# Three unused matmuls in the RWKV recurrence, fp32 low-rank weights kept in SBUF, and the low parts' stores moved to another queue

## The chip, the cores and the metric

The kernel runs on one core of one Trainium2 chip. The metric is device time in microseconds (us) of one execution; less is better. The core's engines are named as the profile names them: PE (TensorE; PEld is its weight load), DVE (VectorE), ACT (ScalarE), POOL (GpSimd) and SP (SyncE). ACTq and SPq are the DMA issues of ACT and SP. PEclk is the granted TensorE clock, 1.00 for 2.4 GHz and 0.50 for 1.2 GHz.

## The reference, cut to what matters

The whole is a two-layer decoder: RWKV-7 time mixing, a feed-forward block, sparse attention, another feed-forward block, over 1024 tokens of width 1024, in float32. Only the time mixing is touched:

```python
xm = x[None] + xx[None] * mix[:, None, None, :]
r, k, v = jnp.einsum('nbsd,nde->nbse', xm[:3], w_rkv)
xv, xw, xa, xg = xm[2], xm[3], xm[4], xm[5]
w_log = -jax.nn.softplus(-(w0 + jnp.tanh(xw @ w1) @ w2)) - 0.5
decay = jnp.exp(-jnp.exp(w_log.astype(f32)))
...
a = jax.nn.sigmoid(a0 + (xa @ a1) @ a2)
g = jax.nn.sigmoid(xg @ g1) @ g2
...
def _wkv7_step(state, inp):
    r_t, w_t, k_t, v_t, a_t, b_t = inp
    sa = jnp.einsum('bhvk,bhk->bhv', state, a_t)
    state = (state * w_t[:, :, None, :] + sa[..., None] * b_t[:, :, None, :]
             + v_t[..., None] * k_t[:, :, None, :])
    y = jnp.einsum('bhvk,bhk->bhv', state, r_t)
    return state, y
```

The kernel does the scan in chunks of 64 tokens: inside a chunk the steps become a triangular system, whose 64x64 matrices (one for each head and chunk) are inverted first.

## The kernel before, in words

**Units.** The time mixing (`rwkv`, about the first 1060 us of the execution) works in four units: two halves of the tokens (hf 0 and 1, 512 tokens each) by two halves of the width (g 0 and 1, 512 columns, 8 heads). In this text a unit is written (hf, g), and they run in the order (0,0), (0,1), (1,0), (1,1). A half begins with `load_x` (tokens loaded and transposed) and `lora1` (the first, narrow factors of the low-rank products, fp32 matmuls, L415). A unit then has `lora2` (the second factors, L517 and L518, a sigmoid on each result by ACT, L519), the projections r, k and v (`proj`), the decays, `prep` (chunk matrices), `invert`, and `wkv` (eight chunks of the recurrence). The generator of each stage is interleaved with others, so that a projection of the next unit runs under the inversion and the recurrence of the one before. The framework's scheduler sets the order on each engine from the order in which the code issues and from its own estimate of times; each engine then works through its list strictly in that order.

**Split precision.** A projection multiplies fp32 data as a high and a low part, each fp32r: ACT casts the raw tile to `hi`, and DVE or POOL computes `lo = raw - hi` (`split`, L54 and L60). Three matmuls (L65, L66, L67) of 128x512 make one product, 12 for each of the 8 contraction steps (kt) of a projection. The weights' tiles are called wr (raw), wh and wl, those of the mixed tokens xm, xmh and xml.

**Kept operands.** `pair` (L436 to L452) makes the two parts the first time and stores them to DRAM if they are needed again: the weights' parts when hf = 0 (for half 1), the tokens' parts when g = 0 (for g = 1). Both stores are issued from ACT's queue (L451), the low part's behind the high part's. When they are needed again, two loads from SP's queue (L445) take the place of load, cast and subtraction. wh, wl, xmh, xml and some tiles of `load_x` and `lora1` share one pool of 14 slots of 128x512 (`u`, with `k.NU` as its size); raw weights have 3 slots (`raw`).

**lora2.** In each unit the columns of w2 and a2 that it needs (128x512 each, 256 KB) are loaded through SP and split like any weight, and the small activations were stacked before by `lora1` as high and low parts over 128 partitions (hw and ha, L419 to L426). Sixteen fp32r matmuls follow, 128x512 each.

**invert.** On DVE, `Lt` (128 partitions by 32x32) is eliminated row by row (L655 and L661), 32 steps of two operations between which DVE takes other work. A MEMSET (L662) writes its diagonal. Then, for each of two halves (sub), DVE transposes the blocks (TX, L666 and the next statement), PE multiplies them in 32 small 32x32 matmuls (xps, L678), ACT copies the result, PE does another 32 (tps, L683), and ACT copies that. `wkv` of the unit follows (its matmuls L717 to L744).

The lines which the prediction's steps touch: the store in `pair` (L451), its reload (L445), the raw weights' load (L124), `lora1` from L418 on, `lora2`, the end of `invert` (L662 to L683), and `k.NU` (14).

Of the kernel before, what the change touches and what calls it, by code (L numbers as in the profile page):

```python
# [7 lines left out]
F32 = mybir.dt.float32  # L8
# [37 lines left out]
def f32(ap):  # L46
    return ap.bitcast(F32)
# [259 lines left out]
def rwkv(k, src, dst):  # L307
# [12 lines left out]
    def t(name, dt=F32):  # L320
        return M_.tile([128, 512], dt, name=name, tag="t", bufs=5)
# [31 lines left out]
    SB = [M_.tile([128, 4, 2, 64], F32, name=f"S{g}") for g in range(2)]  # L353
    for z in SB:
        nc.gpsimd.memset(z, 0.0)
    halo = M_.tile([128, 8], F32, name="halo")
    nc.gpsimd.memset(halo, 0.0)
    st = {}
# [39 lines left out]
    def lora1(hf):  # L398
        xT = st[hf]["xT"]
        a = [acc("la") for _ in range(4)]  # L400
        for kt in range(KT):
            xx = t("xx")
            nc.vector.tensor_tensor(xx, xT[:, kt, 0:512], xT[:, kt, 1:513], ALU.subtract)
            w = raw("wl1")[:, :288]
            nc.sync.dma_start(w, k.w_l1[kt * 128 : (kt + 1) * 128, :])
            xm = {}
            for n in (3, 4, 5):
                xm[n] = u("xm")
                c = V_MIX + 8 * n + kt
                nc.vector.scalar_tensor_tensor(  # L410
                    xm[n], xx, k.vec[:, c : c + 1], xT[:, kt, 1:513], ALU.mult, ALU.add
                )

            for b, n, c0, c1, p0 in ((0, 3, 0, 64, 0), (1, 4, 64, 128, 64), (2, 5, 128, 256, 0), (3, 5, 256, 288, 96)):
                nc.tensor.matmul(  # L415
                    a[b][p0 : p0 + c1 - c0], w[:, c0:c1], xm[n], start=kt == 0, stop=kt == KT - 1
                )
        hw = M_.tile([128, 512], F32R, name="hw", tag="hw", bufs=1)  # L418
        tw = t("tw")  # L419
        nc.scalar.activation(tw[:64], a[0][:64], AF.Tanh)  # L420
        nc.scalar.copy(hw[:64], tw[:64])
        nc.vector.tensor_tensor(hw[64:], tw[:64], f32(hw[:64]), ALU.subtract)
        ha = M_.tile([128, 512], F32R, name="ha", tag="ha", bufs=1)
        nc.scalar.copy(ha[64:], a[1][64:])
        nc.vector.tensor_copy(ha[:64], a[1][64:])
        nc.vector.tensor_tensor(ha[64:], a[1][64:], f32(ha[64:]), ALU.subtract)  # L426
        tg = t("tg")
        nc.scalar.activation(tg, a[2], AF.Sigmoid)
        nc.sync.dma_start(gsc[hf, 0:128], tg)
        tg2 = t("tg2")  # L430
        nc.scalar.activation(tg2[96:], a[3][96:], AF.Sigmoid)
        nc.sync.dma_start(gsc[hf, 128:160], tg2[96:])
        st[hf].update(hw=hw, ha=ha)

    ahead = {}
    PF = [CFG['pf0'], CFG['pf1'], CFG['pf2']]  # L436
# [3 lines left out]
    def pair(key, make, again):  # L440

        if key in kept:
            hi, lo = u(key[0] + "h", F32R), u(key[0] + "l", F32R)
            for i, x in enumerate((hi, lo)):
                nc.sync.dma_start(f32(x), kept[key][i])  # L445
            return hi, lo
        hi, lo = make()
        if again:
            kept[key] = DR.tile([2, 128, 512], F32, name="kept_" + "_".join(map(str, key)))
            for i, x in enumerate((hi, lo)):  # L450
                nc.scalar.dma_start(kept[key][i], f32(x))  # L451
        return hi, lo  # L452

    def operands(hf, n, g, kt):
# [45 lines left out]
    def lora2(hf, g):  # L500

        h_ = st[hf]
        AR = P_.tile([128, 4, 1024], F32, name="AR", tag="AR", bufs=2)
        BK = P_.tile([128, 4, 1024], F32, name="BK", tag="BK", bufs=1)
        s = un[hf, g] = dict(AR=AR, BK=BK)
        if CFG["pfl"] == "b":
            prefetch(hf, 0, g, 1)
        w2 = wtile(k.w_w2[:, g * 512 : (g + 1) * 512], lo_eng=CFG["l2"])
        a2 = wtile(k.w_a2[:, g * 512 : (g + 1) * 512], lo_eng=CFG["l2"])
        if CFG["pfl"] == "a":  # L510
            prefetch(hf, 0, g, 1)
        for i in range(4):
            p = 4 * g + i
            sl = slice(i * 128, (i + 1) * 128)
            for o, w, h, v0 in ((v2(BK[:, i, :512]), w2, h_["hw"], V_W0), (slot(AR[:, i], 0), a2, h_["ha"], V_A0)):
                ps = acc("l2")
                nc.tensor.matmul(ps, w[0][:, sl], h, start=True, stop=False)  # L517
                nc.tensor.matmul(ps, w[1][:, sl], h, start=False, stop=True)  # L518
                s["last"] = nc.scalar.activation(o, v2(ps), AF.Sigmoid, bias=k.vec[:, v0 + p : v0 + p + 1])  # L519

    def decays(hf, g):
# [119 lines left out]
    def invert(hf, g):  # L641
# [10 lines left out]
        for j in range(1, 31):  # L652
# [7 lines left out]
            )  # L660
            nc.vector.tensor_tensor(Lt[:, j + 1 :, :j], Lt[:, j + 1 :, :j], tv, ALU.add)  # L661
        nc.vector.memset(Lt.rearrange("p a b -> p (a b)")[:, 0:1024:33], 1.0)  # L662
        for sub in range(2):
            L = Ln[sub]
            TX = w4("TX", [128, 32, 32])
            nc.vector.transpose(  # L666
                TX[64:96].rearrange("p n j -> p j n"), Lt[64 * sub : 64 * sub + 32].rearrange("p i j -> p j i")
            )
            for b in range(2):
                q = slice(64 + 32 * b, 96 + 32 * b)  # L670
                nc.vector.transpose(
                    L[q, :, 32 * b : 32 * b + 32].rearrange("p n i -> p i n"),
                    Lt[64 * sub + 32 * b : 64 * sub + 32 * b + 32],
                )
            for o in (0, 16):
                ps = (mi if o else ud)("xps").rearrange("p (n i) -> p n i", i=32)
                for n in range(16):
                    nc.tensor.matmul(ps[96:, n], L[64:96, o + n, 32:64], TX[64:96, o + n], start=True, stop=True)  # L678
                CP(k, CFG["cT"])(TX[96:, o : o + 16], ps[96:])
            for o in (0, 16):  # L680
                ps = (mi if o else ud)("tps").rearrange("p (n i) -> p n i", i=32)
                for n in range(16):
                    nc.tensor.matmul(ps[64:96, n], TX[96:, o + n], L[96:, o + n, 32:64], start=True, stop=True)  # L683
                CP(k, CFG["cM"])(L[64:96, o : o + 16, 32:64], ps[64:96])
# [1245 lines left out]
def setup(tc, args, es):  # L1930
    k = Ctx()
    k.tc, k.nc = tc, tc.nc
    for n, a in zip(_INS, args):
        setattr(k, n, a)
    k.NU = 14
    k.psum = k.rows = None
    k.dram = es.enter_context(tc.tile_pool(name="scratch", bufs=1, space=bass.MemoryType.DRAM))
    C = es.enter_context(tc.tile_pool(name="consts", bufs=1, reuse_waits="tile"))
    k.ident = C.tile([128, 128], F32, name="ident")
    k.nc.sync.dma_start(k.ident, k.c_ident)  # L1940
    k.vec = C.tile([128, V_END], F32, name="vec")
    k.nc.sync.dma_start(k.vec, k.vecs)
    k.mhalf = C.tile([128, 16], F32, name="mhalf")
    k.nc.gpsimd.memset(k.mhalf, -0.5)
    return k
# [41 lines left out]
```

## Time and profile before

| | us |
|---|---|
| median of three runs | 3228.42 |
| lowest and highest | 3226.88 and 3240.63 |
| the profiled execution, its own time | 3233.26 |
| its span in the trace | 3231.4 |
| PE busy in the span | 2864.5 (89%) |
| DVE, POOL, ACT busy | 2455.2, 1518.1, 1377.4 |

The profiled execution is one run among others; its time is 4.84 us above the median of the three. The granted clock is 0.924 of full speed in the mean. A row of the timeline reads: start, duration (both us), engine, line, operation, output and inputs, shape, count, and in brackets the idle time of the engine before it with what ended that idle time. A busy PE can still be slow, since a stretch at the granted clock 0.50 counts as busy too; so the clock of a stretch is read beside its busy time.

### The profile page before, as it was taken

What the parts mean: (1) busy time and instruction counts of PE and PEld (TensorE: products, weight loads), DVE (VectorE), ACT (ScalarE), POOL (GpSimd) and SP (SyncE); (2) the same over time, 40 slices, a digit from 0 to 9 for tenths busy, and PEclk for the clock granted to TensorE, in tenths of its full rate; (3) what the DMA queues carried; (4) which work ended last, traced back from release to release, by engine and by line L of the source; (5) the groups of instructions that cost most, each with busy time, mean ns of one, the idle gap of its engine ahead of it and who ended that gap; (6) DMA issues with size and microseconds to landing.
All of it is one profiled execution on the core that took longest, in us unless ns stands there. A gap on an engine that the chain in (4) does not pass through costs nothing. (4 is left out here: it accounts for less than half of the span.)

```text
span 3231.4 us, 41664 instructions
## 1 busy us (share of the span) xinstructions
PE 2864.5 (89%) x15032; PEld 2246.0 (70%) x15032; DVE 2455.2 (76%) x3925; ACT 1377.4 (43%) x2363; POOL 1518.1 (47%) x987
## 2 busy tenths in 40 slices
PE   7689889989897899999698888888998899999788
PEld 3468657777675677777576766566787677777577
DVE  5486767766756788888976689997475888888975
ACT  3433234322322544444223577775363544444331
POOL 2433215222144667766767522212313677766766
PEclk9788978879898999999889889999999999999899
DMA  5554533534325222235212521112214222235212
GB/s 178 198 199 141 189 108 113 181 135 161 121 86 179 82 79 79 78 92 207 78 66 73 182 69 54 45 33 101 80 43 163 61 78 79 79 98 202 78 52 91
DMA packets 236224, 356.44 MB, mean 110 GB/s; under 512 B 17290, under 2 KB 110858, under 8 KB 235634
## 3 DMA queue, kind: packets, MB, share of 16 engines
q1 hardware_dynamic: 208370, 303.44, 29.3%
q10 hardware_dynamic: 27648, 50.34, 4.1%
q8 instruction: 118, 1.93, 0.3%
q14 instruction: 88, 0.72, 0.1%
HBM read 250.57 MB, written 103.15 MB: 109 GB/s over the span
## 5 line engine op out<-in xcount | busy, mean ns | idle before, releaser
L60 POOL TENSOR_TENSOR wo<-wr,wo 128x512 fp32r<-128x512 f32 x220 | 410.8, 1891 | 288.8 <-ACT wo L54 288.8
L1050 DVE SCALAR_TENSOR_TENSOR cv<-u,vec,cv 128x1023 f32<-128x1023 f32 (+1 forms) x176 | 348.2, 1996 | 52.9 <-ACT cv L1045 51.1
L65 PE MATMUL dn<-dh 128*128 128x512 f32 x532 | 219.4, 412 | 68.5 <-DVE acc L1177 68.4
L60 POOL TENSOR_TENSOR dl<-raw,dh 128x1024 fp32r<-128x1024 f32 x82 | 221.1, 2719 | 101.4 <-ACT dh L54 101.1
L65 PE MATMUL p<-xT,wo 128*128 128x512 f32 x528 | 213.4, 404 | 25.3 <-ACT u L1034 19.0
L66 PE MATMUL dn<-dl,dh 128*128 128x512 f32 x532 | 218.1, 410 | 15.2 <-POOL dl L60 7.7
L67 PE MATMUL dn<-dh,dl 128*128 128x512 f32 x532 | 215.9, 406 | 0.0
L1045 ACT ACTIVATE cv<-u,vec 128x1024 f32<-128x1024 f32 x88 | 109.5, 1244 | 248.8 <-DVE u L1039 248.2
L1682 POOL TENSOR_TENSOR cm<-sc,toep 128x256 f32<-128x256 f32 x96 | 75.7, 794 | 297.1 <-DVE mn L1698 228.5
L67 PE MATMUL p<-xT,wo 128*128 128x512 f32 x528 | 208.7, 395 | 5.1 <-POOL wo L60 5.1
L66 PE MATMUL p<-xT,wo 128*128 128x512 f32 x528 | 208.6, 395 | 3.0 <-DVE xT L60 3.0
L1177 DVE SCALAR_TENSOR_TENSOR acc<-acc,dn 128x512 f32<-128x512 f32 x196 | 130.8, 679 | 86.7 <-PE dn L67 86.7
L60 POOL TENSOR_TENSOR wo<-S,wo 128x512 fp32r<-128x512 f32 x88 | 175.6, 2014 | 30.3 <-ACT wo L54 30.3
L54 ACT CAST dh<-raw 128x1024 fp32r<-128x1024 f32 x95 | 94.8, 1047 | 198.0 <-PE dn L67 80.7
L65 PEld LDWEIGHTS dn<-dh 128*128 128x128 f32 x532 | 105.7, 199 | 98.0 <-DVE acc L1177 42.5
L60 POOL TENSOR_TENSOR wl<-wr,wh 128x512 fp32r<-128x512 f32 x56 | 76.6, 1367 | 199.2 <-ACT wh L54 118.5
L65 PEld LDWEIGHTS p<-xT,wo 128*128 128x128 f32 x528 | 100.6, 190 | 63.6 <-ACT u L1034 34.2
L65 PE MATMUL p<-x,wo 128*128 128x512 f32 x352 | 138.8, 394 | 2.8 <-DVE x L60 2.3
L54 ACT CAST wo<-wr 128x512 fp32r<-128x512 f32 x220 | 127.0, 618 | 29.1 <-POOL wo L60 18.7
L54 ACT CAST wh<-wr 128x512 fp32r<-128x512 f32 x108 | 66.6, 621 | 169.8 <-DMA wr<-in_w_w_dram 51.6
L66 PE MATMUL p<-x,wo 128*128 128x512 f32 x352 | 138.4, 393 | 0.0
L65 PE MATMUL pa<-xmh,wh 128*128 128x512 f32 x256 | 106.1, 439 | 36.3 <-ACT xmh L54 32.2
(422 smaller groups left out, 8685.9 us busy)
## 6 DMA issues: line engine op xcount, KB each, us to landing
wr<-in_w_up_dram SPq DMA_DIRECT2D x88, 512.0 KB, 5.9
hd<-cv SPq DMA_DIRECT2D x44, 512.0 KB, 3.4
raw<-hd SPq DMA_DIRECT2D x19, 1024.0 KB, 5.0
raw<-in_w_down_dram SPq DMA_DIRECT2D x19, 1024.0 KB, 7.7
wr<-in_w_wo_dram SPq DMA_DIRECT2D x68, 256.0 KB, 2.9
wr<-in_w_rkv_dram SPq DMA_DIRECT2D x48, 256.0 KB, 3.4
kept_w<-wh ACTq DMA_DIRECT2D x48, 256.0 KB, 2.2
kept_w<-wl ACTq DMA_DIRECT2D x48, 256.0 KB, 3.7
```

What stands on the lines that cost most here:

```text
L54: nc.scalar.copy(hi, raw)
L60: eng.tensor_tensor(lo, raw, f32(hi), ALU.subtract)
L65: mm(ps, lhs[0], rhs[0], start=start, stop=False, **kw)
L66: mm(ps, lhs[0], rhs[1], start=False, stop=False, **kw)
L67: mm(ps, lhs[1], rhs[0], start=False, stop=stop, **kw)
L1045: nc.scalar.activation(o, u, AF.Identity, bias=k.vec[:, cb : cb + 1], scale=k.vec[:, cw[2] : cw[2] + 1])
L1050: nc.vector.scalar_tensor_tensor(o[:, d:], u[:, : 1024 - d], k.vec[:, cw[j] : cw[j] + 1], o[:, d:], ALU.mult, ALU.add)
L1177: nc.vector.scalar_tensor_tensor(o, o, ALPHA if first else 1.0, ps, ALU.mult, ALU.add)
L1682: (nc.vector if CFG["cm"][h4] == "v" else nc.gpsimd).tensor_tensor(cm[:, :near], mk, toep[g][:, h % 8, 256 - near :], ALU.add)
```

## The change

It has three parts, all in `rwkv`.

In `invert`, after the MEMSET of the diagonal, three fp32 matmuls of 128x512 multiply a piece of `Lt` with another piece of it, into the PSUM bank that xps takes next. Nothing reads their result. They need only the MEMSET, and xps needs the transposes and the bank.

In `lora1` and `lora2`, w2 and a2 are loaded once, at the start, 64 partitions each, into one fp32 tile `wa2` that stays. The activations stay whole (`h`, fp32, 64 partitions for each of the two products), and eight fp32 matmuls of 64x128 by 64x512 take the place of sixteen of fp32r. The loads, casts and subtractions of w2 and a2 in each unit, and the stacking, are gone. One slot of the pool `u` is given up (14 to 13).

In `pair`, the store of the low part is issued from SP's queue, that of the high part stays on ACT's.

```diff
+    wa2 = M_.tile([128, 1024], F32, name="wa2")
+    nc.sync.dma_start(wa2[:64], k.w_w2[:64])
+    nc.sync.dma_start(wa2[64:], k.w_a2[64:])
...
-        hw = M_.tile([128, 512], F32R, name="hw", tag="hw", bufs=1)
-        tw = t("tw")
-        nc.scalar.activation(tw[:64], a[0][:64], AF.Tanh)
-        nc.scalar.copy(hw[:64], tw[:64])
-        nc.vector.tensor_tensor(hw[64:], tw[:64], f32(hw[:64]), ALU.subtract)
-        ha = M_.tile([128, 512], F32R, name="ha", tag="ha", bufs=1)
-        nc.scalar.copy(ha[64:], a[1][64:])
-        nc.vector.tensor_copy(ha[:64], a[1][64:])
-        nc.vector.tensor_tensor(ha[64:], a[1][64:], f32(ha[64:]), ALU.subtract)
+        h = M_.tile([128, 512], F32, name="h", tag="h", bufs=1)
+        nc.scalar.activation(h[:64], a[0][:64], AF.Tanh)
+        nc.scalar.copy(h[64:], a[1][64:])
...
-                nc.scalar.dma_start(kept[key][i], f32(x))
+                (nc.scalar, nc.sync)[i].dma_start(kept[key][i], f32(x))
...
-        w2 = wtile(k.w_w2[:, g * 512 : (g + 1) * 512], lo_eng=CFG["l2"])
-        a2 = wtile(k.w_a2[:, g * 512 : (g + 1) * 512], lo_eng=CFG["l2"])
...
-                nc.tensor.matmul(ps, w[0][:, sl], h, start=True, stop=False)
-                nc.tensor.matmul(ps, w[1][:, sl], h, start=False, stop=True)
+                nc.tensor.matmul(ps, wa2[q, 128 * p : 128 * p + 128], h_["h"][q], start=True, stop=True)
...
+        rest, flat = ud("rest"), Lt.rearrange("p a b -> p (a b)")
+        for _ in range(3):
+            nc.tensor.matmul(rest, flat[:, :128], flat[:, :512], start=True, stop=True)
...
-    k.NU = 14
+    k.NU = 13
```

PE's list at the inversion of unit (0,1); pa is the r projection of unit (1,0). Before:

```order
L66 MATMUL pa<-xml,wh 128x512
L67 MATMUL pa<-xmh,wl 128x512
L65 MATMUL pa<-xmh,wh 128x512
L66 MATMUL pa<-xml,wh 128x512
L678 MATMUL xps<-TX,MA 32x32 x32
L67 MATMUL pa<-xmh,wl 128x512
```

After, in the same place (L507 is the fp32 matmul of `lora2`, L655 the new one, L671 is xps):

```order
L507 MATMUL l_3267<-h,wa_133 128x512
L507 MATMUL l_3270<-h,wa_133 128x512
L65 MATMUL pa<-xmh,wh 128x512 x4
L66 MATMUL pa<-xml,wh 128x512
L67 MATMUL pa<-xmh,wl 128x512
L66 MATMUL pa<-xml,wh 128x512
L67 MATMUL pa<-xmh,wl 128x512
L655 MATMUL rest<-Lt 128x512 x3
L671 MATMUL xps<-TX,MA 32x32 x32
```

Besides the three matmuls, the scheduler has moved the inversion forward against the projection: 8 matmuls pa stand between the last one of `lora2` and the inversion, where before there were 35, so that 27 now come behind it.

DVE's list at the same time, where `lora1` of half 1 ends (L655 and L661 before, L644 and L650 after, are the elimination; L60 is the low part of w2; xm, ltmp, Lt as above). Before:

```order
L60 TENSOR_TENSOR wl_3295<-wr_3294,wh_3296 128x512 [waits DMAHW3_49,PE_49,Activation_49]
L655 TENSOR_TENSOR ltmp_3370<-Lt_3365 128x238
L661 TENSOR_TENSOR Lt_3365<-Lt_3365,ltmp_3370 128x17x14 [waits DVE_49]
L425 CAST ha_3282<-la_3162 64x512 [waits Activation_49]
L422 TENSOR_TENSOR hw_3277<-tw_3278,hw_3277 64x512 [waits Activation_49]
L426 TENSOR_TENSOR ha_3282<-la_3162,ha_3282 64x512
L655 TENSOR_TENSOR ltmp_3370<-Lt_3365 128x240 [waits DVE_49]
```

After:

```order
L644 TENSOR_TENSOR ltmp_3305<-Lt_3300 128x238
L650 TENSOR_TENSOR Lt_3300<-Lt_3300,ltmp_3305 128x14x17 [waits DVE_49]
L644 TENSOR_TENSOR ltmp_3305<-Lt_3300 128x234 [waits DVE_49]
L650 TENSOR_TENSOR Lt_3300<-Lt_3300,ltmp_3305 128x13x18 [waits DVE_49]
L644 TENSOR_TENSOR ltmp_3305<-Lt_3300 128x228 [waits DVE_49]
L650 TENSOR_TENSOR Lt_3300<-Lt_3300,ltmp_3305 128x12x19 [waits DVE_49]
```

The subtraction that waited for w2, and the three operations of the stacking, no longer stand among the steps of the elimination.

SP's list in unit (0,1), where the tokens' parts that unit (0,0) stored are loaded again (L445 before, L442 after; L124 is a raw weight's load, L448 a low part's store). Before:

```order
L445 DMA xmh<-kept_xm_0_0_399 128x512 [waits DMAHW2_49,DMAHW1_49,PE_49]
L445 DMA xml<-kept_xm_0_0_399 128x512 [waits DMAHW7_49,DMAHW3_49,Pool_49]
L124 DMA wr<-in_w_rkv_dram 128x512 [waits DMAHW4_49,Pool_49]
L124 DMA wr<-in_w_rkv_dram 128x512 [waits DMAHW6_49,DMAHW5_49,Pool_49]
L445 DMA xmh<-kept_xm_0_1_430 128x512 [waits DMAHW1_49,PE_49]
L445 DMA xml<-kept_xm_0_1_430 128x512 [waits DMAHW7_49]
```

After:

```order
L442 DMA xmh<-kept_xm_0_0_376 128x512 [waits DMAHW6_49,DMAHW1_49,PE_49]
L448 DMA kept_w_1_0_2166<-wl 128x512 [waits DMAHW7_49,Pool_49]
L442 DMA xml<-kept_xm_0_0_376 128x512 [waits DMAHW0_49,PE_49]
L124 DMA wr<-in_w_rkv_dram 128x512 [waits DMAHW2_49,Activation_49]
L442 DMA xmh<-kept_xm_0_1_407 128x512 [waits DMAHW3_49,PE_49]
L448 DMA kept_w_1_1_2191<-wl 128x512 [waits DMAHW4_49,Pool_49]
L442 DMA xml<-kept_xm_0_1_407 128x512 [waits DMAHW5_49,PE_49]
```

A store that waits for POOL's (or DVE's) subtraction now stands ahead of the reload of xml and of the next raw weight's load. In unit (0,0) 48 such stores have moved to SP, in (0,1) and (1,0) 24 each, in (1,1) none.

## Rows read from the trace of the kernel before

**Rows 1.** The page: busy time of PE over the span, and the granted clock in 40 equal slices (about 81 us each).

```profile
PE 2864.5 (89%) x15032; PEld 2246.0 (70%) x15032; DVE 2455.2 (76%) x3925; ACT 1377.4 (43%) x2363; POOL 1518.1 (47%) x987
...
PEclk9788978879898999999889889999999999999899
```

**Rows 2.** Busy time of each engine in three stretches: the loads at the very start, the r projection and the k projection of unit (0,0). Columns: stretch, its length, busy us of PE, PEld, DVE, ACT and POOL (each with its instructions), granted clock, share of the 16 DMA engines, GB/s.

```profile
5.00:10.00 5.00, 3.69 (x16) 3.02 (x16) 0.82 (x2) 1.18 (x2) 0.00 (x0) 1.00 0.96 296
...
55.00:80.00 25.00, 18.32 (x69) 11.88 (x67) 8.40 (x9) 9.95 (x16) 12.22 (x10) 1.00 0.79 271
110.00:140.00 30.00, 24.31 (x83) 16.74 (x83) 8.99 (x10) 11.77 (x19) 13.43 (x11) 0.89 0.82 282
```

**Rows 3.** Timeline of ACT and POOL in the projections of unit (0,0): the weight cast that begins a step, first and last of the r projection read here (six steps apart), one step of it in full, first and last of the k projection (seven steps apart).

```profile
52.61 0.62 ACT L54 CAST wh<-wr 128x512 fp32r<-128x512 f32 x1 [0.50 <-DVE xml L60]
...
66.43 0.62 ACT L54 CAST wh<-wr 128x512 fp32r<-128x512 f32 x1 [1.81 <-POOL xml L60]
67.13 1.30 POOL L60 TENSOR_TENSOR wl<-wr,wh 128x512 fp32r<-128x512 f32 x1 [1.10 <-ACT wh L54]
68.46 0.36 ACTq L451 DMA_DIRECT2D kept_w<-wl  x1
71.29 0.62 ACT L54 CAST wh<-wr 128x512 fp32r<-128x512 f32 x1 [1.82 <-POOL xml L60]
...
81.07 0.62 ACT L54 CAST wh<-wr 128x512 fp32r<-128x512 f32 x1 [1.75 <-POOL xml L60]
111.18 0.62 ACT L54 CAST wh<-wr 128x512 fp32r<-128x512 f32 x1 [1.57 <-POOL xml L60]
142.86 0.62 ACT L54 CAST wh<-wr 128x512 fp32r<-128x512 f32 x1 [1.05 <-DVE xml L60]
```

**Rows 4.** What ACT waited for between 41 and 145 us: waiting operation, releaser, us in total, times, longest.

```profile
ACT wh L54 <- POOL xml L60: 23.8, 14, 2.8
ACT xmh L54 <- DMA kept_w<-wh: 7.3, 4, 1.9
```

**Rows 5.** Costs around the low-rank products of half 0: the fp32 matmuls of `lora1` in the timeline (records, not matmuls) and all of its records, the cast that waits for w2, two of `lora2`'s fp32r matmuls in a row, two of its sigmoids in a row.

```profile
14.92 23.20 PE L415 MATMUL la<-xm,wl 128*64 128x512 f32 x60 [1.99 <-issue]
L415 PE MATMUL la<-xm,wl x128: 592/617/1222, 14.9 to 427.7; 128*64 128x512 f32 x64, 128*128 128x512 f32 x32, 128*32 128x512 f32 x32
37.25 0.62 ACT L54 CAST wh<-wr 128x512 fp32r<-128x512 f32 x1 [24.41 <-DMA wr<-in_w_w_dram]
43.79 0.40 PE L518 MATMUL l<-hw,wl 128*128 128x512 f32 x1
44.02 0.40 PE L517 MATMUL l<-ha,wh 128*128 128x512 f32 x1
47.24 0.72 ACT L519 ACTIVATE BK<-l,vec 128x512 f32<-128x512 f32 x1
47.81 0.73 ACT L519 ACTIVATE AR<-l,vec 128x512 f32<-128x512 f32 x1
```

**Rows 6.** Timeline at the end of `lora1` of half 1, under the elimination of unit (0,1): ACT's cast of w2, DVE's low part of it, one operation of the stacking, and the MEMSET that ends the elimination.

```profile
424.82 0.62 ACT L54 CAST wh<-wr 128x512 fp32r<-128x512 f32 x1 [27.19 <-DMA wr<-in_w_w_dram]
425.47 0.69 DVE L60 TENSOR_TENSOR wl<-wr,wh 128x512 fp32r<-128x512 f32 x1 [6.16 <-ACT wh L54]
428.20 0.69 DVE L422 TENSOR_TENSOR hw<-tw,hw 64x512 fp32r<-64x512 f32 x1
457.21 0.09 DVE L662 MEMSET Lt<- 128x32 f32 x1
```

**Rows 7.** The four inversions, (0,0), (0,1), (1,0) and (1,1): three stretches with the columns of rows 2, the first xps of each with PE's idle time before it, the MEMSETs of the last two units, and the first L744 of `wkv` in (0,1) and (1,1), which is the end of its first chunk.

```profile
236.00:246.00 10.00, 6.86 (x73) 5.66 (x72) 8.63 (x9) 2.30 (x4) 2.06 (x3) 0.50 0.53 203
461.00:492.00 31.00, 31.00 (x320) 26.39 (x318) 11.07 (x9) 8.30 (x14) 2.55 (x2) 0.51 0.21 69
666.00:704.00 38.00, 32.90 (x358) 28.73 (x359) 16.77 (x23) 5.51 (x10) 0.23 (x1) 0.51 0.14 45
...
239.15 1.05 PE L678 MATMUL xps<-TX,MA 32*32 32x32 f32 x16 [3.14 <-DVE TX L666]
459.93 1.26 PE L678 MATMUL xps<-TX,MA 32*32 32x32 f32 x34 [3.27 <-DVE TX L666]
668.38 0.09 DVE L662 MEMSET Lt<- 128x32 f32 x1
671.10 1.11 PE L678 MATMUL xps<-TX,MA 32*32 32x32 f32 x17 [8.79 <-DVE TX L666]
856.27 0.09 DVE L662 MEMSET Lt<- 128x32 f32 x1
860.05 1.16 PE L678 MATMUL xps<-TX,MA 32*32 32x32 f32 x26 [2.70 <-DVE TX L666]
...
491.51 0.47 PE L744 MATMUL sps<-UV,MA 64*64 64x64 f32 x2
887.60 0.47 PE L744 MATMUL sps<-UV,MA 64*64 64x64 f32 x2
```

**Rows 8.** The reloads of kept operands (L445), over all units: one of those who waited for them (us, times), and time from issue to landing. Last, a wait of ACT in unit (1,0), between 540 and 600 us.

```profile
  PE pa L65: 5.9, 5
...
DMA to landing us min/median/max: 2.5/4.0/6.3
...
ACT xmh L54 <- POOL xml L60: 7.5, 3, 3.6
```

More of the change, by code (lines that the diff above doesn't have):

```diff
@@ L432, in lora1 @@
         nc.sync.dma_start(gsc[hf, 128:160], tg2[96:])
-        st[hf].update(hw=hw, ha=ha)
+        st[hf].update(h=h)
     ahead = {}
@@ L505, in lora2 @@
         s = un[hf, g] = dict(AR=AR, BK=BK)
-        if CFG["pfl"] == "b":
-            prefetch(hf, 0, g, 1)
-        w2 = wtile(k.w_w2[:, g * 512 : (g + 1) * 512], lo_eng=CFG["l2"])
-        a2 = wtile(k.w_a2[:, g * 512 : (g + 1) * 512], lo_eng=CFG["l2"])
-        if CFG["pfl"] == "a":
-            prefetch(hf, 0, g, 1)
         for i in range(4):
             p = 4 * g + i
-            sl = slice(i * 128, (i + 1) * 128)
-            for o, w, h, v0 in ((v2(BK[:, i, :512]), w2, h_["hw"], V_W0), (slot(AR[:, i], 0), a2, h_["ha"], V_A0)):
+            for o, q, v0 in ((v2(BK[:, i, :512]), slice(0, 64), V_W0), (slot(AR[:, i], 0), slice(64, 128), V_A0)):
                 ps = acc("l2")
-                nc.tensor.matmul(ps, w[0][:, sl], h, start=True, stop=False)
-                nc.tensor.matmul(ps, w[1][:, sl], h, start=False, stop=True)
+                nc.tensor.matmul(ps, wa2[q, 128 * p : 128 * p + 128], h_["h"][q], start=True, stop=True)
                 s["last"] = nc.scalar.activation(o, v2(ps), AF.Sigmoid, bias=k.vec[:, v0 + p : v0 + p + 1])
```

## The prediction

> **What bounds the kernel now.** I read the page first. PE is busy 89% of the span, at a granted clock that dips in the slices of the first third [rows 1]. The change touches nothing behind the RWKV stage, so only its four units are read further, each by the wait that ends last there.
>
> Unit (0,0), its projections: PE is idle in a fifth to a quarter of the time, and the DMA engines are at a share of 0.79 and 0.82 [rows 2]. The timeline shows why: ACT casts the weight at 66.43, POOL subtracts until 68.43, ACT issues the low part's store at 68.46 because that store waits for POOL and stands in ACT's list; the tokens follow in the same way, and the next weight's cast comes at 71.29, "released by POOL's xml" [rows 3]. A step takes (81.07 - 52.61) / 6 = 4.74 us in r and (142.86 - 111.18) / 7 = 4.53 us in k [rows 3], and ACT's weight casts alone waited 23.8 us for POOL [rows 4]. This stretch is paced by the issue of low-part stores.
>
> Inversions: PE waits for DVE's transposes, 2.70 to 8.79 us before the first xps, and then works at half clock: 31.00 of 31 us busy at 0.51 in unit (0,1), 32.90 of 38 in (1,0) [rows 7]. Here PE's clock and the chain PE-ACT-PE set the pace.
>
> End of lora1 in half 1: ACT's cast of w2 waited 27.19 us for its load, DVE's low part of w2 stood 6.16 us behind it, and the elimination of unit (0,1) stood behind that on DVE [rows 6].
>
> **The change part by part.** The sum is made against the profiled execution, 3233.26 us, and 4.84 is taken off at the end for the median of the three runs. Negative is faster.
>
> **Stores of the low part on SP, unit (0,0).** ACT no longer waits for a subtraction; the store waits in SP's list instead, behind which stand raw weights that are needed some steps later. What is late next is the DMA: a step moves one weight in and four parts out, 5 x 256 KB = 1.31 MB. At the best rate seen, 296 GB/s [rows 2], that is 4.43 us; by the shares of this stretch it is 4.74 x 0.79 = 3.75 and 4.53 x 0.82 = 3.71 us. So the gain lies between 6 x 0.31 + 7 x 0.10 = 2.6 and 6 x 0.99 + 7 x 0.82 = 11.7 us. I take the middle, **-7**: the rate at the start was reached with reads alone, and the stretch itself has the mixture that counts.
>
> Here the Trainium skill speaks against the change ("Trainium Kernel Development and Optimization", Key Constraints): DMAs issued by SP, ACT and POOL run on the same 16 DMA engines, and issuing from several saves only the issue time. By it the 13 steps would gain two issues of 0.36 us each at most, about 9 us, and nothing where the engines are full. Row 68.46 shows that what ACT loses is mostly its wait in order ahead of the issue, which the rule leaves out; I keep the term from the rows.
>
> **Start.** Three ACT casts on the path to the first projection go (w2, a2, hw), 3 x 0.62 = -1.9 [rows 5]. The eight fp32 matmuls are slower: L415 has 128 records for the 64 matmuls of the code, so 60 records in 23.20 us are 0.77 us a matmul, 8 x 0.77 = 6.2 us, where eight sigmoids at a spacing of 0.57 take 4.6 [rows 5]; +1.6 if none runs ahead, +0.8 taken. The two loads of wa2 (0.52 MB) stand ahead of the tokens' loads, in a stretch with a DMA share of 0.96 at 296 GB/s [rows 2]: +1.8. Sum **+0.7** (-3 to +3).
>
> **Three matmuls in each inversion.** At full clock they take 3 x 0.77 = 2.3 us, under PE's idle time of 2.70 to 3.27 us in three of the units [rows 7], so they cost nothing there; if they come at half clock they take 4.6. What a full clock in the first part of an inversion is worth I read from two units: from MEMSET to the end of the first chunk (0,1) takes 491.51 - 457.21 = 34.3 us [rows 6, 7], all at half clock, and (1,1), which comes back to full speed in between, 887.60 - 856.27 = 31.3 [rows 7]. So -3.5 for (0,1), and -2.5 for (1,1), which has half of it already. In (1,0) PE has idled 8.79 us by the first xps and is at half clock already, the three take 4.6 us where 671.10 - 668.38 = 2.7 are free, +1.9, less the 3.5: -1.6. In (0,0) the clock is at 0.50 from 236 on, 4.6 us where 3.1 are free, +1.5, less 2: -0.5. Sum **-8** (+6.4 if all four run at half clock and nothing comes back, about -27 for a clock that stays up).
>
> **Resident low-rank weights in the other units.** In (1,0)'s lora2, DVE loses the wait of 6.16 and five operations of 0.69 (3.45), so the MEMSET of (0,1) can come up to 9.6 us sooner [rows 6]. But 27 matmuls of the r projection now stand behind the inversion; at a spacing of 0.23 us [rows 5] that is 6.2 us of PE work, and the stretch into which it goes has PE busy for 31.00 of 31 us [rows 7]. Net -3.4 (0 to -9.6). The other two calls lose two subtractions of 0.69 each on DVE, half of them on the path: -1.4. Eight fp32 matmuls take 6.2 us for 16 x 0.23 = 3.7 us: +2.5 in each of three calls where PE sets the pace, nothing where the two halves of the array overlap or PE waits anyway; one call is charged, +2.5. Sum **-2.3** (-11 to +8).
>
> **Stores ahead of reloads.** In (0,1) and (1,0) 24 steps each have a store on SP that waits for a subtraction. Behind it in SP's list stand the reload of xml (in (0,1)) and raw weights; PE waits for the reloaded parts. Before, such waits cost PE's L65 5.9 us in five places [rows 8]; five waits longer by an issue of 0.36 are +2. ACT is free of POOL in (1,0), where it waited 7.5 us for xml [rows 8]; -2 of it, since PE is paced by other things there. Sum **0** (-5 to +15).
>
> **13 slots for 14.** In unit (0,0) ACT waited 7.3 us for a slot whose store had not landed [rows 4]; one slot in 14 fewer lengthens that. **+1.5** (0 to +7.3).
>
> Together -7 + 0.7 - 8 - 2.3 + 0 + 1.5 = -15.1: 3218.2 for the execution, **3213.3** for the median. A change of 0.5%, 16.1 us, is about what a measurement of this kernel can tell from none, so "faster" begins under 3212.3 and "slower" over 3244.6.
>
> **The rivals.**
>
> *The clock falls anyway (the three matmuls don't do what they are there for).* PE at 0.51 was busy without a gap for 31 us in (0,1) [rows 7]: small 32x32 matmuls did not bring the clock back, so it may fall again in the next stretch of small matmuls. Then the term is +3 (two units pay 1.5 and 1.9) in place of -8: 3224. Against it: (1,1) does come back for a while.
>
> *The clock stays up.* With no idle gap ahead of xps, the stretches at half clock in (0,1) and (1,0) would run at full speed. PE's 31.0 + 32.9 us [rows 7] would shrink by half at most, 32; as ACT's copies lie in the chain, -27 over all units in place of -8: 3194. For it: the gap is the one thing all four have in common.
>
> The Trainium skill has this rule ("TensorE: Matmul & The Clock Gate", HAM oscillation): idle gaps on PE bring the half rate, and its remedy is to leave none. The trace agrees on the gaps, and does not on busy stretches: 31.00 of 31 us were busy at 0.51.
>
> *The DMA engines are the bound of unit (0,0).* Steps stay at 4.4 to 4.5 us: -2.6 in place of -7, 3218.
>
> *SP's list is the new wait (slower).* Place: unit (0,1), where each of 24 steps has a store between the reload of xmh and that of xml. If the reload has no lead over its use, each step pays POOL's 1.30 [rows 3] and an issue of 0.33 to 0.36, 24 x 1.63 = +39: 3252. It decides from (3244.6 - 3213.3) / 24 = 1.3 us a step on. Against it: a reload lands in 4.0 us and only five were waited for [rows 8], so loads have a lead of more than a step now.
>
> **How the numbers follow.** Forecast as summed, within 10 us either way: 0.42, of which half lies under 3212.3. Clock stays up: 0.24, all faster. Clock falls anyway: 0.13, and DMA the bound: 0.09, both within 0.5%. SP's list: 0.10, slower. Other terms at their slow ends, still within 0.5%: 0.02. So faster 0.21 + 0.24 = 0.45; same 0.21 + 0.13 + 0.09 + 0.02 = 0.45; slower 0.10. The range reaches from below the case of the full clock with room for the first term's -11.7, 3185, to the case of the falling clock with the slots' +7.3 and a few reloads late, 3235.
>
> **What would show it.** Steps of (0,0): weight casts 3.8 to 4.4 us apart, and no wait of ACT for POOL; if they stay at 4.5 with a DMA share over 0.9, the engines were the bound. Inversions: granted clock 1.00 from the MEMSET of (0,1) and (1,1) over some 8 us, a first chunk ending some 31 us behind the MEMSET in (0,1); the second half of the inversion at 0.5 again if the forecast is right, at 1.0 if the rival is. Lora1 of half 1: no gap of 6 us on DVE, MEMSET of (0,1) 5 to 10 us sooner against the start of the unit. SP: waits of PE for xml out of reloads, five before; twenty of over 1 us would make me wrong. What would make the sum wrong above all is a new order that leaves PE idle ahead of an inversion, since 27 matmuls that filled that time now stand behind it.

## The result and the profile after

| | before | after |
|---|---|---|
| median of the runs beside each other, us | 3227.65 (4 runs) | 3182.72 (4 runs) |
| lowest and highest | 3223.84, 3240.63 | 3175.82, 3186.95 |
| ratio to before, 95% interval | | 0.9852 [0.9819, 0.9885] |
| the profiled execution, its span | 3233.26, 3231.4 | 3186.95, 3185.1 |

The kernel became 45 us faster. The forecast was 3213.3, its range 3185 to 3235: the direction was right, the size was three times too small, and the time lies 2.3 us under the range. Among the chances "within 0.5%" had as much as "faster", 0.45.

Where the 45 us went can be read along the recurrence: at the four MEMSETs that end the eliminations, and at the last L744 (L737 after) of the stage. Both columns are one profiled execution each.

| us from the start of the span | MEMSET (0,0) | (0,1) | (1,0) | (1,1) | last of wkv |
|---|---|---|---|---|---|
| before | 236.06 | 457.21 | 668.38 | 856.27 | 946.3 |
| after | 212.56 | 416.93 | 624.08 | 815.40 | 901.2 |
| difference | -23.5 | -40.3 | -44.3 | -40.9 | -45.1 |

The first MEMSET and the five records whose last one ends the stage, before and after:

```profile
236.06 0.09 DVE L662 MEMSET Lt<- 128x32 f32 x1
946.03 0.46 PE L744 MATMUL sps<-UV,MA 128*64 128x64 f32 x5
...
212.56 0.09 DVE L651 MEMSET Lt<- 128x32 f32 x1
900.98 0.46 PE L737 MATMUL sps<-UV,MA 128*64 128x64 f32 x5
```

So 23.5 us come before the first inversion, another 17 between the first and the second, and little behind that. The rest of the program is the same code and moved the span by 1 us.

The projections of unit (0,0) in the changed kernel answer to [rows 2 to 4]. Busy time in two stretches (columns as in rows 2), the weight casts of step 1 of r and of step 0 of k, seven steps apart, and what ACT waited for most, in total, between 41 and 145 us:

```profile
52.00:80.00 28.00, 22.25 (x87) 15.60 (x88) 21.86 (x19) 18.23 (x31) 19.13 (x14) 1.00 0.96 345
110.00:140.00 30.00, 26.60 (x96) 20.58 (x94) 13.71 (x17) 14.53 (x25) 15.94 (x11) 0.69 0.65 240
...
49.73 0.66 ACT L54 CAST wh<-wr 128x512 fp32r<-128x512 f32 x1
73.20 0.62 ACT L54 CAST wh<-wr 128x512 fp32r<-128x512 f32 x1
...
ACT xmh L54 <- DMA kept_xm<-xml: 8.5, 6, 2.4
```

The reader should see three things. The weight cast no longer names POOL as its releaser. A step takes (73.20 - 49.73) / 7 = 3.35 us, where it took 4.74. And what ACT waits for now is the landing of a store that holds a slot: the wait has moved to the DMA engines, which are at 0.96 and 345 GB/s.

The end of the low-rank products of half 1 answers to [rows 6]: what DVE waited for there, and the end of the elimination of (0,1).

```profile
403.46 0.75 DVE L588 SCALAR_TENSOR_TENSOR pr<-AR,vec,BK 128x512 f32<-128x512 f32 x1 [4.79 <-DMA gsc<-tg]
409.24 0.19 DVE L594 COPY bon<-bp 128x32 f32<-128x32 f32 x1 [4.36 <-PE bp L536]
416.93 0.09 DVE L651 MEMSET Lt<- 128x32 f32 x1
```

The wait for the cast of w2 is gone. DVE still waits 4.79 us for a load (gsc) and 4.36 us for PE, but later, when most of the elimination is done.

The inversions answer to [rows 7]: the three unused matmuls in (0,0), (0,1), (1,0) and (1,1) (six records each time), the matmul next to them, and the first L737 of (0,1) and (1,1).

```profile
212.70 4.54 PE L655 MATMUL rest<-Lt 128*128 128x512 f32 x6 [3.12 <-DVE Lt L651]
217.17 1.00 PE L671 MATMUL xps<-TX,MA 32*32 32x32 f32 x26
...
417.08 0.63 PE L66 MATMUL pa<-xml,wh 128*128 128x512 f32 x1
417.50 0.63 PE L67 MATMUL pa<-xmh,wl 128*128 128x512 f32 x1
417.93 4.57 PE L655 MATMUL rest<-Lt 128*128 128x512 f32 x6
422.44 0.75 PE L671 MATMUL xps<-TX,MA 32*32 32x32 f32 x18
...
624.22 5.49 PE L655 MATMUL rest<-Lt 128*128 128x512 f32 x6 [4.97 <-DVE Lt L651]
629.63 0.53 PE L671 MATMUL xps<-TX,MA 32*32 32x32 f32 x9
...
816.54 3.25 PE L655 MATMUL rest<-Lt 128*128 128x512 f32 x6
...
444.58 0.27 PE L737 MATMUL sps<-UV,MA 64*64 64x64 f32 x1
842.71 0.37 PE L737 MATMUL sps<-UV,MA 64*64 64x64 f32 x1
```

The matmuls have two records each. They take 3.25 to 5.49 us, not 2.3: they run largely at half clock. In (0,1) the projection's matmuls just ahead of them come at a spacing of 0.43 us, which is the half clock already. The first chunk ends 444.58 - 416.93 = 27.7 us behind its MEMSET, where it was 34.3, and in (1,1) 842.71 - 815.40 = 27.3, where it was 31.3. Looked at alone, this would seem to bear out the step of the prediction on these matmuls; the experiments show that it doesn't.

### The profile page after: what moved, and what is told of

Read it like the earlier page. It is cut to its first block, busy times and chain, and to the rows that moved or that the text cites. A ratio compares the mean times of both kernels' runs of the same rounds, so it can differ in the third digit from the quotient of the medians.

```text
span 3185.1 us, 41741 instructions
## 1 busy us (share of the span) xinstructions
PE 2853.7 (90%) x15056; PEld 2227.6 (70%) x15056; DVE 2447.8 (77%) x3911; ACT 1368.5 (43%) x2353; POOL 1528.5 (48%) x987
## 5 line engine op out<-in xcount | busy, mean ns | idle before, releaser
L60 POOL TENSOR_TENSOR wo<-wr,wo 128x512 fp32r<-128x512 f32 x220 | 412.2, 1897 | 287.0 <-ACT wo L54 287.0
L60 POOL TENSOR_TENSOR dl<-raw,dh 128x1024 fp32r<-128x1024 f32 x82 | 220.2, 2708 | 100.3 <-ACT dh L54 87.3
L60 POOL TENSOR_TENSOR wo<-S,wo 128x512 fp32r<-128x512 f32 x88 | 176.7, 2025 | 29.2 <-ACT wo L54 29.2
L60 POOL TENSOR_TENSOR wl<-wr,wh 128x512 fp32r<-128x512 f32 x56 | 76.9, 1374 | 184.6 <-ACT wh L54 111.9
L65 PE MATMUL p<-x,wo 128*128 128x512 f32 x352 | 138.9, 395 | 2.0 <-DVE x L60 1.5
L66 PE MATMUL p<-x,wo 128*128 128x512 f32 x352 | 138.3, 393 | 0.0
L67 PE MATMUL p<-x,wo 128*128 128x512 f32 x352 | 137.9, 392 | 0.0
L66 PEld LDWEIGHTS dn<-dl,dh 128*128 128x128 f32 x532 | 107.2, 202 | 36.9 <-DVE dl L60 8.0
```

The lines of the kernel that those rows point to most:

```text
L60: eng.tensor_tensor(lo, raw, f32(hi), ALU.subtract)
L65: mm(ps, lhs[0], rhs[0], start=start, stop=False, **kw)
L66: mm(ps, lhs[0], rhs[1], start=False, stop=False, **kw)
L67: mm(ps, lhs[1], rhs[0], start=False, stop=stop, **kw)
```

## The experiments

All times are medians of several runs; a ratio compares with runs of the kernel before on the same chip. The experiments first make each part of the change alone, then take one back.

**One part alone: the stores.**

```diff
-                nc.scalar.dma_start(kept[key][i], f32(x))
+                (nc.scalar, nc.sync)[i].dma_start(kept[key][i], f32(x))
```

> The kernel before with one edit: the low parts' stores issued from SP's queue. Theory (the stores carry most of the gain, through unit (0,0)): the first MEMSET comes about 20 us sooner (before 236.06, so about 216) and the time is 3200 to 3207. Rival (the gain of unit (0,0) needs the three parts together, the stores give only the 7 us of the prediction): 3220, first MEMSET at 229. Rival (reloads behind stores on SP cost later what is won first): first MEMSET at 216, but the time over 3215.

Measured: 3200.89, ratio 0.9904 [0.9886, 0.9922]. Some 31 us (by the ratio) of the 45 to 48 come with this one line. The stretch of the r projection in its trace, the stretch behind it, two weight casts, the four MEMSETs, and the records that end the stage:

```profile
52.00:80.00 28.00, 23.83 (x91) 17.98 (x92) 20.32 (x15) 16.85 (x28) 21.54 (x16) 0.94 0.99 366
84.00:98.00 14.00, 2.65 (x10) 1.58 (x8) 10.51 (x11) 5.77 (x11) 11.19 (x11) 0.65 0.27 95
...
53.28 0.65 ACT L54 CAST wh<-wr 128x512 fp32r<-128x512 f32 x1
...
76.66 0.62 ACT L54 CAST wh<-wr 128x512 fp32r<-128x512 f32 x1
...
216.07 0.09 DVE L662 MEMSET Lt<- 128x32 f32 x1
434.62 0.09 DVE L662 MEMSET Lt<- 128x32 f32 x1
633.07 0.09 DVE L662 MEMSET Lt<- 128x32 f32 x1
826.95 0.09 DVE L662 MEMSET Lt<- 128x32 f32 x1
920.96 0.46 PE L744 MATMUL sps<-UV,MA 128*64 128x64 f32 x5
```

The two casts shown are seven casts apart, 3.34 us each. The engines are full (0.99), and being full they move 366 GB/s here. The first MEMSET comes 20 us sooner than before, as the first theory had it, the next two 22.6 and 35.3. In the units where reloads stand behind stores, (0,1) and (1,0), nothing is given back. Behind the third MEMSET some 10 us are: the fourth is 29.3 us sooner and the end of the stage 25.1, so that 5 us are left beyond the 20. The profiled execution took 3209.69 us, the slowest of the six, and its span is only 23.5 us under that of the kernel before. Where the rest of the 31 us lies can't be read from it.

**One part alone: the resident fp32 weights** (the edits of lora1, lora2 and `k.NU` of the change, without the other two parts).

> The kernel before with one edit: w2 and a2 resident in fp32, 13 slots, eight fp32 matmuls in each lora2. Theory: 3 us won at the start and 7 to 9 us at the end of the low-rank products of half 1 (the wait of DVE for the cast of w2 is gone), time 3214 to 3219. Rival (fp32 matmuls and the lost slot eat it): 3226 to 3232. Rival (the resident weights carry the gain between the first and the second MEMSET, 17 us): 3205 to 3210, second MEMSET 17 us or more nearer to the first than before (221.2 us apart before).

Measured: 3212.33, ratio 0.9938 [0.9921, 0.9955], some 20 us. Two of its MEMSETs, and DVE's waits of over 2 us between 370 and 446 us:

```profile
233.65 0.09 DVE L651 MEMSET Lt<- 128x32 f32 x1
440.94 0.09 DVE L651 MEMSET Lt<- 128x32 f32 x1
...
421.64 0.75 DVE L588 SCALAR_TENSOR_TENSOR pr<-AR,vec,BK 128x512 f32<-128x512 f32 x1 [5.00 <-DMA gsc<-tg]
426.90 0.19 DVE L594 COPY bon<-bp 128x32 f32<-128x32 f32 x1 [4.19 <-PE bp L536]
```

It wins 2.4 us up to the first MEMSET and another 13.9 up to the second, near to the third theory, which had 17; the time lies between the first theory (3214 to 3219) and the third (3205 to 3210). The rival of costly fp32 matmuls falls. Up to the first two MEMSETs this part and the stores add up to nearly what the whole change won: 2.4 + 20.0 for 23.5 us, 16.3 + 22.6 for 40.3.

**One part alone: the unused matmuls.**

```diff
+        rest, flat = ud("rest"), Lt.rearrange("p a b -> p (a b)")
+        for _ in range(3):
+            nc.tensor.matmul(rest, flat[:, :128], flat[:, :512], start=True, stop=True)
```

> The kernel before with one edit: the three unused matmuls in each inversion. Theory (they hold or bring back the clock for the first half of an inversion): 3217 to 3222, granted clock 1.00 in the 8 us from the first xps of (0,1), first L744 of (0,1) 30 to 32 us behind the MEMSET (34.3 before). Rival (the clock falls anyway): 3227 to 3231. Rival (the clock stays up through the inversion): 3205 or less.

Measured: 3229.41, ratio 0.999 [0.9977, 1.0003]: nothing that can be told from zero, and 8 us would lie outside. Yet the clock came back. Its trace at (0,0) and (0,1): the MEMSETs, the matmuls, the first xps, and the end of the first chunk; behind it the MEMSET of (1,0) and the records that end the stage, and last the end of the first chunk of (0,0) in the kernel before:

```profile
236.94 0.09 DVE L662 MEMSET Lt<- 128x32 f32 x1
237.08 5.49 PE L666 MATMUL rest<-Lt 128*128 128x512 f32 x6 [5.03 <-DVE Lt L662]
242.50 0.68 PE L682 MATMUL xps<-TX,MA 32*32 32x32 f32 x9
271.43 0.37 PE L748 MATMUL sps<-UV,MA 64*64 64x64 f32 x1
...
468.42 0.09 DVE L662 MEMSET Lt<- 128x32 f32 x1
468.56 4.53 PE L666 MATMUL rest<-Lt 128*128 128x512 f32 x6 [3.30 <-DVE Lt L662]
473.02 1.16 PE L682 MATMUL xps<-TX,MA 32*32 32x32 f32 x31
...
476.00:500.00 24.00, 24.00 (x310) 20.32 (x308) 11.64 (x13) 7.01 (x12) 2.37 (x3) 0.79 0.19 68
...
495.69 0.34 PE L748 MATMUL sps<-UV,MA 64*64 64x64 f32 x1
...
668.10 0.09 DVE L662 MEMSET Lt<- 128x32 f32 x1
937.37 0.46 PE L748 MATMUL sps<-UV,MA 128*64 128x64 f32 x5
...
265.67 0.47 PE L744 MATMUL sps<-UV,MA 64*64 64x64 f32 x2
```

In (0,1) the granted clock from 476 to 500 us is 0.79, where it was 0.51 in the like stretch [rows 7], and the first chunk ends 27.3 us behind the MEMSET, not 34.3. But the MEMSET itself comes at 468.42 where it came at 457.21, and in (0,0) the first xps is 5.6 us behind the MEMSET (3.1 before) and the first chunk ends 4.9 us later behind it. A reason for part of it stands in PE's list: the scheduler puts 332 projection matmuls ahead of the first xps where before there were 340, and 603, 930 and 1198 for 611, 938 and 1211 in the other units. The three unused matmuls take the place of 8 to 13 useful ones, which then run behind the inversion, where PE is busy. At the spacings of 0.23 and 0.43 us that is 1.8 to 5.6 us in each unit. The 11 us do not last: the MEMSET of (1,0) is back at the time that it had before (668.38), and the stage ends 8.7 us sooner in this one execution, while the span is 2.9 us shorter. The same code behind the stage takes 2282 to 2298 us in the kept traces, so a few us of a single trace decide nothing; the ratio of twelve runs does.

**One part taken back: the unused matmuls.** The changed kernel without the three lines above.

> The changed kernel without the three unused matmuls. Theory (they are worth about 8 us beside the other parts as well): 3188 to 3193, against 3182.7. Rival (the gain is in the other two parts alone): 3181 to 3184. Rival (they are worth the half-clock stretches of two units): 3200 or more.

Measured: 3180.03, ratio 0.9841 [0.9821, 0.9861]. The interval lies within that of the changed kernel: there, too, the three matmuls bring nothing that shows. The shorter first chunk of (0,1) does not need them either. Its MEMSET, the end of its first chunk, and the stretch between them from 419 us on:

```profile
411.36 0.09 DVE L651 MEMSET Lt<- 128x32 f32 x1
436.25 0.27 PE L733 MATMUL sps<-UV,MA 64*64 64x64 f32 x1
...
419.00:437.00 18.00, 17.60 (x296) 15.10 (x294) 13.44 (x13) 8.55 (x14) 2.84 (x2) 1.00 0.36 119
```

The chunk ends 24.9 us behind the MEMSET, against 27.7 with the matmuls, and the clock is 1.00 without them. Here their removal puts 8 to 11 projection matmuls back ahead of each xps (345, 595, 927, 1209, against 337, 584, 919, 1198).

**Six of them.** `range(3)` becomes `range(6)`.

> The changed kernel with six unused matmuls in each inversion in place of three. Theory (the three took 3.3 to 5.5 us each time, at half clock, and delayed the first xps by 1.5 to 2.5 us, which the clock that they bring back pays; three more delay it by 2.4 us at full clock with nothing to win): +8 to +12, 3190 to 3195. Rival (more work in front holds the clock longer): 3170 to 3180.

Measured: 3206.11, ratio 0.9938 [0.9916, 0.996]. About 28 us slower than the changed kernel, by ratios, beyond the 8 to 12 of the theory; that more such work would hold the clock is refuted. So they are not free under the transposes.

**The stores on SP in the first unit alone.**

```diff
-                (nc.scalar, nc.sync)[i].dma_start(kept[key][i], f32(x))
+                (nc.scalar, nc.sync if first else nc.scalar)[i].dma_start(kept[key][i], f32(x))
```

(`first` is true in unit (0,0).)

> The changed kernel, with the low parts' stores on SP's queue in unit (0,0) alone; in (0,1) and (1,0) they go back to ACT's queue. Theory (the stores gain some 20 us in unit (0,0) and a few more in the other two units, since ACT is free there too): 3186 to 3192, against 3182 for the changed kernel. Rival of the prediction (in (0,1) and (1,0) stores on SP hold up reloads): faster than the changed kernel, 3170 to 3178. Rival (the stores gain as much outside (0,0)): over 3195.

Measured: 3189.94, ratio 0.9868 [0.984, 0.9895], against 0.9852 for the changed kernel. The two can't be told apart; a loss by reloads waiting on SP, which would have made this version faster, does not show.

**Both stores on SP.** `nc.sync.dma_start(kept[key][i], f32(x))` for both parts.

> The changed kernel with the high parts' stores on SP's queue as well. Theory (what counted was ACT's wait for a subtraction, and the high part's store waits for nothing on ACT): 3180 to 3190, no gain, perhaps a loss of some us by two issues more for each step on SP. Rival (ACT's issue time is what the stores cost): 3165 to 3175.

Measured: 3200.79, ratio 0.9906 [0.9885, 0.9926], slower than the changed kernel, and by more than the theory's "some us": 17 by ratios. In its trace PE waits 16.5 us for reloaded operands, in four places, where in the changed kernel it waits 10.8 us in six and before the change 7.8 in eight. That SP's list is what makes this version slower fits these waits; that they are the whole of the 17 us is not shown.

**Twelve slots.** `k.NU = 12`.

> The changed kernel with 12 slots in the pool u in place of 13. Theory (a slot is held until its store has landed, and ACT now waits for such slots in unit (0,0), so one fewer costs 3 to 8 us): 3186 to 3191. Rival (slots are no limit): 3180 to 3184.

Measured: 3194.99, ratio 0.99 [0.9874, 0.9925], above the 3186 to 3191 of the theory: some 15 us by ratios, though the interval still touches that of the changed kernel.

**Thirteen slots in the kernel before.** `k.NU = 13`, nothing else.

> The kernel before with 13 slots in the pool u in place of 14, nothing else. Theory (slots limit how far projections' operands run ahead; one fewer cost the changed kernel some 13 us between 13 and 12): 3236 to 3246. Rival (in the kernel before ACT's wait for POOL is the limit, so a slot is worth little): 3228 to 3233, as the prediction's 1.5 us had it.

Measured: 3238.1, ratio 1.0032 [1.0013, 1.0052]: a slot costs 10 us there, nearly seven times the term of the prediction. The 20 us of the resident weights are what is left after it. If the two simply add, they are worth some 30 without it; that is an estimate, since the slots of the changed kernel need not cost the same.

**fp32 weights loaded in each lora2.**

```diff
-    wa2 = M_.tile([128, 1024], F32, name="wa2")
-    nc.sync.dma_start(wa2[:64], k.w_w2[:64])
-    nc.sync.dma_start(wa2[64:], k.w_a2[64:])
...
+        wa2 = M_.tile([128, 512], F32, name="wa2", tag="wa2", bufs=2)
+        nc.sync.dma_start(wa2[:64], k.w_w2[:64, g * 512 : (g + 1) * 512])
+        nc.sync.dma_start(wa2[64:], k.w_a2[64:, g * 512 : (g + 1) * 512])
```

> The changed kernel, but w2 and a2 are not resident: each lora2 loads its 64x512 of each in fp32 through SP where the kernel before did, without cast or subtraction. Theory (the gain of the low-rank part is that ACT and DVE no longer stand in order behind these loads): the same as the changed kernel, 3178 to 3187, for only PE waits for the load now. Rival (the gain is the loads that are gone, and their places in SP's list): 3192 to 3202.

Measured: 3176.92, ratio 0.9839 [0.9816, 0.9862]. The rival falls: that the weights are resident is worth nothing that shows. What helps is that they are no longer split, with all that hangs on it.

**Before, with a raw tile of their own for w2 and a2** (13 slots).

```diff
+    def rawl(name):
+        return P_.tile([128, 512], F32, name=name, tag="rawl", bufs=1)
...
-        w2 = wtile(k.w_w2[:, g * 512 : (g + 1) * 512], lo_eng=CFG["l2"])
-        a2 = wtile(k.w_a2[:, g * 512 : (g + 1) * 512], lo_eng=CFG["l2"])
+        w2 = wsplit(k, u, k.w_w2[:, g * 512 : (g + 1) * 512], 512, CFG["l2"], rawl)
+        a2 = wsplit(k, u, k.w_a2[:, g * 512 : (g + 1) * 512], 512, CFG["l2"], rawl)
```

> The kernel before with 13 slots in u (as the run before, 1.0032 of the kernel before), and a raw tile of their own for w2 and a2, so that their loads no longer wait for the three raw slots that lora1's weights pass through. Casts, subtractions and sixteen fp32r matmuls stay. Theory (what the resident weights gained is the end of ACT's and DVE's waits in order for these loads, 24 and 27 us on ACT, 6 us on DVE in front of the elimination): at least 9 us under the kernel with 13 slots, 3220 to 3229, no wait of DVE over 2 us ahead of the low part of w2 in half 1. Rival (it is the work itself that is gone, casts, subtractions, stacking and half of the matmuls): 3234 to 3242.

Measured: 3241.11, ratio 1.0039 [1.0017, 1.0061], as with 13 slots alone. In half 1, ACT's cast of w2 and the next cast on DVE:

```profile
424.88 0.62 ACT L54 CAST wh<-wr 128x512 fp32r<-128x512 f32 x1 [17.26 <-PE la L418]
...
436.23 0.69 DVE L428 CAST ha<-la 64x512 fp32r<-64x512 f32 x1 [5.60 <-ACT ha L427]
```

The wait for the load is gone and another stands in its place: the cast now waits 17.26 us for lora1's matmuls, at the same time as before (424.82), and on DVE the stacking waits 5.60 us for ACT, for lora1's sums, in the same place among the steps of the elimination where the low part of w2 waited 6.16 us [rows 6]. So this run does not separate the work from the waits as it was meant to; what it does show is that freeing these loads from the raw slots alone gains nothing, since the cast and the stacking wait for lora1 all the same.

**Fourteen slots beside reloaded fp32 weights,** with one tile of 512 columns (`bufs=1`, `k.NU = 14`), and the same without the unused matmuls.

> The changed kernel with w2 and a2 loaded in fp32 in each lora2 into one tile of 512 columns, and the space so freed used for a 14th slot. Theory (a slot is worth more than 3 us, reloading costs nothing): 3165 to 3175. Rival (13 slots are enough, only 12 are too few): 3176 to 3184.

> The same with 14 slots, and without the three unused matmuls. Theory (they cost what they bring): within 5 us of the run with them. Rival (they are worth 8 us where the rest of the chain is shorter): 8 us or more above it.

Measured: 3195.15, ratio 0.9889 [0.9864, 0.9915], and without the matmuls 3172.7, ratio 0.982 [0.9795, 0.9845]. The 14th slot gives nothing that shows: neither theory of the first holds, since it is slower than both said, and by ratios 16 us slower than the version with reloaded weights and 13 slots; why is open. The three matmuls cost 22 us here, and the intervals do not touch. The version without them has the lowest ratio of all, but its interval overlaps that of the changed kernel, so that it beats the kernel before and not, by these runs, the changed one.

## Why the prediction was right or wrong

**Stores of the low part.** The mechanism was right, and the size failed: -7 forecast, some 31 us measured alone, 20 of them before the first MEMSET. The step that failed is the floor of the DMA: "at the best rate seen, 296 GB/s" a step would take 4.43 us, and by the shares of the stretch 3.75. The single-part run moved 366 GB/s at a share of 0.99, and a step took 3.34 us, less than 1.31 MB / 366 GB/s = 3.58. The rate of the loads at the start was no ceiling for this mixture. And a step need not last as long as its own transfers: at 3.34 us a step the projection runs ahead of its stores, as far as the slots allow, and the stretch behind r, with a DMA share of 0.27 from 84 to 98 us, has room for those that are left. Fourteen steps at 1.2 to 1.4 us make the 17 to 20 us. The end of the range, -11.7, was a bound from rows that did not bound it. The other 11 us are not placed. The term for the later units was 0, with ACT's 7.5 us of waits [rows 8] valued at 2; the trace of the part alone shows 5 us more at the end of the stage than at the first MEMSET, and taking the later units' stores back to ACT cost 5 us by ratios, which can't be told from none.

**The issue of a store.** By the rule of the Trainium skill ("Trainium Kernel Development and Optimization", Key Constraints) at most about 9 us, by the prediction's estimate, were to be had; the runs disagree with that, 31 us. The engines are shared, as it says, and they did become the bound (a share of 0.99), but the place where a store waits counted for more than its issue.

**Start.** The first projection matmul comes at 48.2 us for 51.5, -3.3 against +0.7 forecast, just past its bound of -3; with the resident weights alone it comes at 50.8.

**Three matmuls.** The value of the clock was about right, and it is seen: first chunks 3 to 7 us shorter in three units of the single-part run. The step that failed is "under PE's idle time ... so they cost nothing there". They ran largely at half clock, 3.2 to 5.5 us long, delayed the first xps by 1.0 to 2.8 us in the changed kernel, and took the place of 8 to 13 projection matmuls in PE's list. And the changed kernel without them has a short first chunk in (0,1) too, at the full clock from 419 us on. Net: ratio 0.999 [0.9977, 1.0003] for -8 forecast. Why the second MEMSET came 11 us later in that run's trace, and the third did not, is only partly explained by this (4.9 us stem from (0,0)); the rest is open. So is how far the 22 us of the version with 14 slots are the matmuls' own time and how far the order that they bring with them, since any edit here makes the scheduler place the projections anew.

**Resident weights.** -2.3 in the other units, +0.7 at the start and +1.5 for the slot, together about 0, forecast; -20 measured. The gain on DVE was seen rightly, up to 9.6 us; what was set against it failed. The elimination of (0,1) from its second step to the MEMSET, before and with the part alone:

```profile
387.20:457.30 70.10, 58.30 (x199) 30.04 (x197) 57.08 (x112) 22.81 (x37) 6.22 (x5) 0.81 0.40 131
...
379.40:441.00 61.60, 53.06 (x189) 23.95 (x188) 50.84 (x104) 18.17 (x30) 5.28 (x4) 0.89 0.35 117
```

It is 8.5 us shorter, and DVE is busy 6.2 us less in it: 3.45 for the five operations that are gone, most of the rest for work that now lies outside the stretch. In all five kept traces with split w2 and a2 this stretch takes 70 to 73 us, in all ten without 58 to 67. The 27 displaced matmuls were charged to this part with 6.2 us; the part alone displaces none of them (612 ahead of the second inversion for 611). Eight fp32 matmuls were charged with 2.5 us more than sixteen fp32r; in the single-part run they took 1.99 + 2.86 = 4.85 us in (0,1), 1.2 more, two records for each matmul:

```profile
203.18 1.99 PE L507 MATMUL l<-h,wa 64*128 64x512 f32 x8
206.44 2.86 PE L507 MATMUL l<-h,wa 64*128 64x512 f32 x8 [1.27 <-ACT BK L508]
```

And the other 5.4 of the 13.9 us between the first two MEMSETs came ahead of the elimination, for which the prediction had no term; up to the start of the k projection of (0,1), behind the first inversion, it was about 8. Busy time there in the kernel before:

```profile
265.00:294.00 29.00, 26.05 (x231) 22.05 (x230) 17.38 (x28) 11.27 (x20) 11.00 (x11) 0.85 0.35 119
```

and in the single-part run:

```profile
265.00:294.00 29.00, 27.76 (x265) 22.15 (x263) 20.78 (x30) 13.54 (x24) 15.87 (x16) 1.00 0.40 137
```

PE has more to do there, at the full clock. What brings that work forward was not tried by itself. That the loads cost nothing is shown by the reloading run. That in the elimination it is DVE's work more than its waits is read from the two stretches above, where DVE's idle time fell by 2.3 us only; the run that was to separate work and waits did not, and for the other 5.4 us the cause is open.

**Stores ahead of reloads, the slower rival.** Rightly given little. Putting the stores back on ACT outside (0,0) gained nothing, and PE's waits for reloaded operands went from eight places and 7.8 us to six and 10.8, far from the twenty waits that were to show the forecast wrong. With both stores on SP they are 16.5 us.

**13 slots.** +1.5 forecast, 10 us measured in the kernel before, outside the term's bounds (0 to 7.3). A wait of 7.3 us "for a slot" [rows 4] was taken as the whole of the pool's influence, in one unit.

The range failed since its low end was built on the full clock, which did not bring the time, and on a bound of the first term that was no bound. That the time missed it by only 2.3 us is luck: the low end came from a clock that stays up, and that did not happen, while the stores and the resident weights brought some 31 and 20 us in place of 7 and nothing.

## What to carry to other kernels

A DMA issue that waits for another engine belongs in the list of an engine that has nothing urgent behind it; price it by what stands behind the wait, over every step, not by its issue. A bandwidth read in one stretch is no ceiling for another mixture of transfers, and with buffers between, a stretch may run faster than its own transfers for as long as the buffers last. Work put into an idle gap to hold a clock has to be weighed with what the scheduler would have put there: here it displaced useful matmuls and the whole gained nothing that shows, and only the runs with that part alone and without it could tell, for the stretch looked better by itself.

## What was not expected of the hardware

The DMA engines moved 366 GB/s at a share of 0.99 in a stretch of weight loads and stores, and 296 at 0.96 in the tokens' loads at the start [rows 2]: the share, not the rate, tells how near the limit is. Six unused matmuls in place of three cost 28 us by ratios over four inversions; the twelve that are added would be 12 x 0.77 = 9 us at full clock and 18 at half by the price of L415 [rows 5].
